# A hybrid pooling / neighbourhood-attention block: the MLP's second-half token operands are written down in three pieces between the early block products instead of in one place

## The chip, the cores and the metric

The kernel runs on one core of one Trainium2 chip. The metric is the device time of one execution in microseconds (us); lower is better. All times inside a run are counted from the start of the span, the stretch from the first to the last instruction that the hardware profiler recorded. The engines are called PE (TensorE matrix products; PEld is its weight load), DVE (VectorE), ACT (ScalarE), POOL (GpSimd) and SP (SyncE, which here only issues transfers).

## The reference

One layer of a diffusion trunk, all in float32, on 1024 tokens of width 1024 with 256 context tokens:

```
h = modulate(rmsnorm(x)); u, q, k, v = h @ w_in
mix = concat(pool_mixer(u), neighbourhood_attention(q, k, v, context)) @ w_out
x = x + gt1 * rmsnorm(mix)
h = modulate(rmsnorm(x), shift2, scale2)             # 1024 x 1024
y = square(relu(h @ w_mlp_in)) @ w_mlp_out           # 1024 x 4096 x 1024
x = x + gt2 * rmsnorm(y)
```

The part around the change is the first MLP product, `h @ w_mlp_in`, and what is just ahead of it.

## The kernel before, in words

Every float32 product is made of three products of rounded operands: an operand is split into a high part (an ACT copy to fp32r, line 143) and a low part (a DVE subtraction, line 144), and `three` (lines 168 to 170) adds high*high, high*low and low*high into one PSUM bank. A split of a 128x1024 page is one ACT cast and one DVE subtraction of that size; a split of a weight tile is one of each, of 128x512.

The first MLP product is done with Strassen's scheme in Winograd's form. The token matrix is cut into four blocks (two token halves, two feature halves) and the weights into four, and seven block products take the place of eight. The token operands have names. `B11` and `B21` come from the first token half (`first_half`). The other five, `T2`, `T1`, `T3`, `B22`, `T4`, need the second token half and are written by `second_half(names)`: two pages each, with subtractions by lines 770 to 775, then a split of each page into `th` (high) and `tl` (low) by `token_part`. In the profile the five carry the names `thT`/`tlT` (for T2, T1, T3, T4) and `thB`/`tlB` (for B22; also for B11 and B21).

The 32 columns of 128 hidden features are worked in 16 pairs p. For p below EARLY = 6 the two products that need only `B11` and `B21` come early: for each group of two pairs, `first_sum` makes x = A11 * B11 in a PSUM bank `phx` (12 matmuls) and copies it to `s1` (line 898, ACT), and `second_sum` adds A12 * B21 into the same bank (12 matmuls more) and squares its positive part (lines 840 and 841, ACT). So the order on PE is x0, x1 with B11, x0, x1 with B21, then the 32 transposes of the second token half (line 737), then x2, x3 and x4, x5 in the same manner. A second sum can't start before its own first sum's copy to `s1` is done, since it changes the bank. After these, `block_pair(p)` does the other five products of a pair, of 12 matmuls each: y with T2 (bank `phy`), z with T1 (`phz`), v with T3 (`phv`), then z with B22 and v with T4 added into their banks. Between z's two products ACT copies the bank out (line 934), and between v's two DVE reads it (line 937). The five weight operands S2, S1, S3, S4, A22 of a pair are made just ahead by `weight_parts`: four DVE combinations (line 813) and five splits.

The order of PE's instructions is fixed by `in_order`. The other engines' queues are ordered when the program is built, by a scheduler that goes by the order in which the code names the instructions and by when it thinks that each can start; the hardware then runs each engine's queue strictly in that order. The instructions of `T2` are held in the written order on ACT and DVE by another `in_order`, and those of block pair 0 may not come before them (`issue_after`). Weight tiles rotate through 8 buffers (`whl`), raw weights through 4 (`wraw`), pages through 33 (`act`), and the small tiles `s1`, `r11`, `u2`, `c22` through 7.

The place of the change:

```
for p in range(0, EARLY, 2):
    ... xs[q], early[q] = first_sum(q) for both q; then second_sum(q, xs[q]) for both
    if p == 0:
        with in_order(ET.Activation, ET.DVE) as made_first:
            second_half(("T2",))
        second_half(("T1", "T3", "B22", "T4"))
```

Of the kernel before, what the change touches and what calls it, by code (L numbers as in the profile page):

```python
# [79 lines left out]
def hybrid_block(ctx, tc, x, ctx_in, w_mod, b_mod, gp1, gp2, w_in, pool_w, rpb, w_out, w1, w2, vectors,  # L80
# [17 lines left out]
    def page(name, dt=F32):  # L98
        return act.tile([P, 1024], dt, tag="pg", name=name)


    @contextmanager
    def in_order(*engines):
        block = nc.cur_bb
        n = len(block.bb.instructions)
        last = {}
        yield last
        assert nc.cur_bb is block
        for i in block.bb.instructions[n:]:
            if i.engine in engines:  # L110
                if i.engine in last:
                    tc.add_manual_dep(i, last[i.engine].name,
                                      mybir.DependencyInfo(mybir.DependencyClass.NoSync, mybir.DependencyReason.DATA),
                                      reason="order")
                last[i.engine] = i
# [564 lines left out]
    with tc.tile_pool(name="ps2", bufs=8, space=PSUM) as ps2:  # L680
# [4 lines left out]
      with ExitStack() as tmp2:  # L685
# [45 lines left out]
        def normal_pair(b, kp, both=True):  # L731
            f = page(f"nf{b}_{kp}")
            for o in range(2):
                k = 2 * kp + o
                pt = bank(f"px{b}_{k}")
                for i in range(4):
                    nc.tensor.transpose(pt[:, i * P : (i + 1) * P], mp1[4 * b + i][:, k * P : (k + 1) * P], ident)
                fo = f[:, o * 512 : (o + 1) * 512]
                if b and o and both:
                    nc.vector.tensor_scalar(fo, pt, a2[:, k : k + 1], s2[:, k : k + 1], mul, add)  # L740
                else:
                    nc.scalar.activation(fo, pt, AF.Identity, bias=s2[:, k : k + 1], scale=a2[:, k : k + 1])
            return f

        def token_part(name, kp, f):
            hi, lo = page(f"th{name}_{kp}", F32R), page(f"tl{name}_{kp}", F32R)
            split(f, hi, lo)
            tok[name, kp] = hi, lo
# [9 lines left out]
        def second_half(names):  # L758
            if not held:
                nf = dict((kp, normal_pair(1, kp, kp % 2 == 0)) for kp in (0, 2, 1, 3))  # L760
                nf = [nf[kp] for kp in range(4)]
                held["b12"], held["B22"] = nf[:2], nf[2:]
                held["T1"], held["T2"] = [[page(f"t{i}_{kp}") for kp in range(2)] for i in (1, 2)]
            b12, b22, b21 = held["b12"], held["B22"], [plain[0, 2 + kp] for kp in range(2)]
            for name in names:
                for kp in range(2):
                    t1, t2 = held["T1"][kp], held["T2"][kp]
                    src = {"T1": t1, "T2": t2, "T3": b12[kp], "B22": b22[kp], "T4": b21[kp]}[name]
                    if name == "T2":
                        nc.vector.tensor_tensor(t1, b12[kp], plain[0, kp], sub)  # L770
                        nc.vector.tensor_tensor(t2, b22[kp], t1, sub)
                    elif name == "T3":
                        nc.vector.tensor_tensor(src, b22[kp], src, sub)
                    elif name == "T4":
                        nc.vector.tensor_tensor(src, src, t2, sub)
                    token_part(name, kp, src)
# [86 lines left out]
        def lookahead(gens, n):  # L863
            ahead = []
            for g in gens:
                for w in g:
                    ahead.append(w)
                    if len(ahead) > n:
                        yield ahead.pop(0)
            yield from ahead  # L870
# [8 lines left out]
        def sequence():  # L879
            for p in range(NPAIR):  # L880
                yield from weight_parts(p, ("S2", "S1", "S3", "S4", "A22") if p < EARLY else
                                        ("A11", "S2", "S1", "S3", "A12", "S4", "A22"))
# [7 lines left out]
        def first_sum(p):  # L890
            x = bank(f"phx{p}")
            step(x, "B11", True)
            if p in (EARLY - 2, EARLY - 1):
                o = (p - EARLY + 2) * 512
                s1 = two_sums[:, o : o + 512]
            else:
                s1 = part(f"s1_{p}")
            nc.scalar.copy(s1, x)  # L898
            return x, s1

        def second_sum(p, x):
            step(x, "B21", False)
            r11 = part(f"r11_{p}")
            squared(x, r11)
            defer(keep, "A11", p, r11)
            return r11
# [13 lines left out]
        def block_pair(p, ahead):  # L920
            sa, sb = page(f"sa{p}"), page(f"sb{p}")
            if p < EARLY:
                s1, r11 = early[p], sb[:, 512:]
                nc.sync.dma_start(r11, kept("A11", p))
            else:
                x, s1 = first_sum(p)
            y = bank(f"phy{p}")
            step(y, "T2", True)
            u2 = part(f"u2_{p}")
            nc.vector.tensor_tensor(u2, y, s1, add)  # L930
            z = bank(f"phz{p}")
            step(z, "T1", True)
            c22 = part(f"c22_{p}")
            nc.scalar.copy(c22, z)
            v = bank(f"phv{p}")
            step(v, "T3", True)
            nc.vector.tensor_tensor(c22, v, c22, add)
            nc.vector.tensor_tensor(c22, c22, u2, add)  # L938
            squared(c22, c22)
            defer(keep, "A22", p, c22)  # L940
            if p >= EARLY:
                r11 = second_sum(p, x)
            ahead()
            step(z, "B22", False)
            c12 = part(f"c12_{p}")
            nc.vector.tensor_tensor(c12, z, u2, add)  # L946
            squared(c12, c12)
            defer(combine_hidden, p, r11, c12, c22, sa, sb)
            ahead()
            step(v, "T4", False)  # L950
            c21 = part(f"c21_{p}")
            nc.vector.tensor_tensor(c21, v, u2, add)
            squared(c21, c21)
            defer(keep, "A12", p, c21)
            defer(combine_last, p, c21, sa, sb)
# [69 lines left out]
        with in_order(ET.PE) as first:  # L1025
            for p in range(0, EARLY, 2):
                both = [q for q in (p, p + 1) if q < EARLY]
                xs = {}
                for q in both:
                    xs[q], early[q] = first_sum(q)  # L1030
                for q in both:
                    second_sum(q, xs[q])
                if p == 0:
                    with in_order(ET.Activation, ET.DVE) as made_first:
                        second_half(("T2",))
                    second_half(("T1", "T3", "B22", "T4"))
            parts = lookahead([sequence()], 4)
            with tc.issue_after(made_first[ET.Activation]), tc.issue_after(made_first[ET.DVE]):
                block_pair(0, lambda: None)
            for p in range(1, NPAIR - 1):  # L1040
                block_pair(p, lambda: None)
# [145 lines left out]
```

## Time and profile before

| | |
|---|---|
| time, median of 3 runs (lowest to highest) | 1126.92 us (1125.63 to 1127.53) |
| profiled execution: its time | 1126.66 us |
| profiled execution: its span | 1124.9 us, 14398 instructions |
| mean granted TensorE clock | 0.985 |
| PE busy | 1075.7 us, 96% |
| DVE busy | 696.4 us, 62% |
| ACT busy | 511.1 us, 45% |
| share of PE in the chain that ended last | 83% |

The busy shares are means over the whole span. The work around the change lies from about 493 us (first early product) to 552 us (end of block pair 0). A timeline row gives the start, the duration, the engine, the line, the operation and its operands and, in brackets, how long the engine had stood idle before and what released it. PE's matmuls are pipelined: one lasts 0.39 us, while a new one starts every 0.227 us. Operations on ACT and DVE overlap in the same way: a 128x512 cast of 0.62 us holds ACT for 0.52 us until the next one starts, a 128x1024 cast of 1.04 us for 0.95 us; a 128x512 subtraction of 0.69 us holds DVE for 0.60 us, one of 128x1024 (1.22 us) for 1.14 us.

### The profile page before, as it was taken

What the parts mean: (1) busy time and instruction counts of PE and PEld (TensorE: products, weight loads), DVE (VectorE), ACT (ScalarE), POOL (GpSimd) and SP (SyncE); (2) the same over time, 40 slices, a digit from 0 to 9 for tenths busy, and PEclk for the clock granted to TensorE, in tenths of its full rate; (3) what the DMA queues carried; (4) which work ended last, traced back from release to release, by engine and by line L of the source; (5) the groups of instructions that cost most, each with busy time, mean ns of one, the idle gap of its engine ahead of it and who ended that gap; (6) DMA issues with size and microseconds to landing.
All of it is one profiled execution on the core that took longest, in us unless ns stands there. A gap on an engine that the chain in (4) does not pass through costs nothing.

```text
span 1124.9 us, 14398 instructions
## 1 busy us (share of the span) xinstructions
PE 1075.7 (96%) x5456; PEld 865.8 (77%) x5456; DVE 696.4 (62%) x1089; ACT 511.1 (45%) x848; POOL 61.6 (5%) x109
## 2 busy tenths in 40 slices
PE   5979999998999999998999999999999999999996
PEld 3667887785677778886888888888878888888885
DVE  4432654624788832579888767675477667556575
ACT  4373112313777732477555455554454334334441
POOL 1020000004220000220000000000000000000001
PEclk9989999998999999998999999999999999999998
DMA  9911863224000001852664535353587666555546
GB/s 285 312 50 37 276 231 113 92 95 143 20 20 2 5 16 48 240 172 75 217 212 165 186 127 173 130 173 112 208 322 277 252 244 223 180 194 187 188 172 202
DMA packets 94265, 179.32 MB, mean 159 GB/s; under 512 B 6898, under 2 KB 39154, under 8 KB 94196
## 3 DMA queue, kind: packets, MB, share of 16 engines
q1 hardware_dynamic: 76644, 144.80, 39.2%
q10 hardware_dynamic: 16272, 29.40, 7.0%
q0 software_dynamic: 1280, 4.21, 1.1%
q8 instruction: 43, 0.70, 0.3%
q14 instruction: 26, 0.21, 0.1%
HBM read 140.62 MB, written 37.76 MB: 159 GB/s over the span
## 4 chain that ended last, share of the span: by engine, by line
PE 83%; DVE 5%; ACT 4%; DMA 4%; issue 2%; POOL 2%; SPq 0%; ACTq 0%; DVEq 0%; POOLq 0%
PE S L586 3%; PE po L650 3%; PE pyv L170 3%; PE pyz L170 3%; PE pyz L169 3%; PE pyv L169 3%; PE pyv L168 3%; PE pyz L168 3%; PE T L624 3%; PE phz L170 3%; PE phz L168 2%; PE phz L169 2%; PE phv L170 2%; PE phv L168 2%; PE phv L169 2%; PE pyx L169 2%
## 5 line engine op out<-in xcount | busy, mean ns | idle before, releaser
L840 ACT ACTIVATE c<-c 128x512 f32<-128x512 f32 x48 | 30.4, 632 | 58.5 <-DVE c L938 24.0
L608 ACT ACTIVATE sp<-sp,nm 128x640 f32<-128x640 f32 (+1 forms) x64 | 51.5, 805 | 11.3 <-DVE nm L600 11.3
L168 PE MATMUL phx<-thB,wpA 128*128 128x512 f32 x128 | 51.1, 400 | 5.6 <-ACT s L898 5.6
L144 DVE TENSOR_TENSOR wpS<-S,wpS 128x512 fp32r<-128x512 f32 x64 | 43.7, 686 | 13.8 <-ACT wpS L143 13.8
L600 DVE CUSTOM_DVE_ANT_0 sp<-S,tab 128x640 f32<-128x640 f32 (+1 forms) x56 | 42.9, 802 | 14.3 <-PE S L586 14.3
L625 ACT COPY pt<-T 128x512 f32<-128x512 f32 x64 | 37.1, 579 | 31.1 <-PE T L624 27.9
L169 PE MATMUL phx<-tlB,wpA 128*128 128x512 f32 x128 | 50.7, 396 | 0.0
L170 PE MATMUL phx<-thB,wpA 128*128 128x512 f32 x128 | 50.5, 395 | 0.0
L143 ACT CAST wpS<-S 128x512 fp32r<-128x512 f32 x64 | 39.3, 615 | 23.3 <-PE phv L170 10.3
L624 PE MATMUL T<-ident,sp 128*128 128x128 f32 x256 | 37.1, 285 | 2.8 <-DVE px L631 2.7
L624 PEld LDWEIGHTS T<-ident,sp 128*128 128x128 f32 x256 | 28.1, 143 | 14.7 <-issue 7.3
L139 POOL TENSOR_TENSOR ry<-vy,nhalf 128x1 f32<-128x1 f32 x8 | 4.4, 550 | 612.1 <-DVE vy L137 612.1
L615 DVE TENSOR_SCALAR sp<-sp,ri 128x640 f32<-128x640 f32 (+1 forms) x64 | 35.4, 553 | 2.3
L586 PE MATMUL S<-kT,q 64*128 64x384 f32 (+1 forms) x128 | 31.9, 525 | 3.2 <-DVE nm L600 3.1
L841 ACT ACTIVATE c<-c 128x512 f32<-128x512 f32 x48 | 30.3, 632 | 10.0 <-DVE sa L911 9.2
L168 PEld LDWEIGHTS phx<-thB,wpA 128*128 128x128 f32 x128 | 24.6, 192 | 11.5 <-ACT s L898 6.4
L713 DVE TENSOR_TENSOR mp<-pw,Ga 128x512 f32<-128x512 f32 x16 | 11.0, 689 | 35.0 <-ACT jo L130 35.0
L946 DVE TENSOR_TENSOR c<-phz,u 128x512 f32<-128x512 f32 x16 | 11.1, 691 | 32.4 <-PE phz L170 32.4
L563 POOL TENSOR_TENSOR tab<-msk,U 128x128 f32<-128x128 f32 x48 | 24.8, 554 | 71.1 <-DMA U<-in_rpb 71.1
L170 PEld LDWEIGHTS phx<-thB,wpA 128*128 128x128 f32 x128 | 24.6, 192 | 5.3
L169 PEld LDWEIGHTS phx<-tlB,wpA 128*128 128x128 f32 x128 | 24.6, 192 | 5.1
L130 ACT ACTIVATE jo<-pw 128x512 f32<-128x512 f32 x16 | 9.6, 598 | 40.4 <-PE pw L170 40.4
(893 smaller groups left out, 3281.3 us busy)
## 6 DMA issues: line engine op xcount, KB each, us to landing
b<-in_w SPq DMA_DIRECT2D x64, 512.0 KB, 4.1
hrS<-hdS SPq DMA_DIRECT2D x32, 512.0 KB, 4.8
hrA<-hdA SPq DMA_DIRECT2D x24, 512.0 KB, 4.7
wm<-in_w_mod SPq DMA_DIRECT2D x16, 512.0 KB, 9.7
wa_0w<-in_w SPq DMA_DIRECT2D x16, 512.0 KB, 4.8
wa_1w<-in_w SPq DMA_DIRECT2D x16, 512.0 KB, 4.2
hdA<-c ACTq DMA_DIRECT2D x32, 256.0 KB, 2.1
hdS<-sa ACTq DMA_DIRECT2D x32, 256.0 KB, 2.9
```

The costliest lines, as they stand in the source:

```text
L143: nc.scalar.copy(hi, src)
L144: nc.vector.tensor_tensor(lo, src, hi.bitcast(F32), sub)
L168: nc.tensor.matmul(ps, ahi, bhi, start=first, stop=False, skip_group_check=more)
L169: nc.tensor.matmul(ps, ahi, blo, start=False, stop=False, skip_group_check=more)
L170: nc.tensor.matmul(ps, alo, bhi, start=False, stop=last, skip_group_check=more)
L586: nc.tensor.matmul(S[e][:, c0 : c0 + keys.shape[1]], q[hs, cols], keys[hs], start=True, stop=True)
L600: nc.vector.tensor_tensor_reduce(out=to, in0=s, in1=bt, scale=1.0, scalar=BIG, op0=add, op1=ALU.min, accum_out=nm)
L608: nc.scalar.activation(sp, sp, AF.Exp, bias=least[i, e], scale=-1.0, accum_out=su)
L615: nc.vector.tensor_scalar_mul(probs[i, e], probs[i, e], ri)
L624: nc.tensor.transpose(t[:, c * P : (c + 1) * P], probs[i, e][:, c * P : (c + 1) * P], ident)
L625: nc.scalar.copy(turns[i][0][:, e], t.rearrange("p (i t) -> p i t", i=4))
L650: nc.tensor.matmul(po[e * HD : (e + 1) * HD, (m % 4) * P : (m % 4 + 1) * P], v[:, f : f + HD], pt[:, e, c] if c < 4 else px[:, e], start=( ...
```

## The change

`second_half` is called three times. After x0 and x1 it writes `T2` only, as before; after x2 and x3 it writes `T1` and `T3`; after x4 and x5 it writes `B22` and `T4`. No instruction is added or taken away, and the pages are handed out in the same order.

```
                 if p == 0:
                     with in_order(ET.Activation, ET.DVE) as made_first:
                         second_half(("T2",))
-                    second_half(("T1", "T3", "B22", "T4"))
+                else:
+                    second_half(("T1", "T3") if p == 2 else ("B22", "T4"))
```

In the built program PE's queue is the same. ACT's queue before, from the cast of T3's second page on (thB22 and thT4 stand for one page each, s4 and s5 for the copies of line 898 of x4 and x5, r4 and r5 for lines 840 and 841 of x4 and x5, "cast S2(0)" for the weight cast of operand S2 of pair 0):

```
before: thT3, cast S2(0), thB22, cast S1(0), thB22, thT4, thT4, s4, s5, cast S3(0), cast S4(0), cast A22(0), r4 840,
        cast S2(1), r4 841, cast S1(1), r5 840, cast S3(1), r5 841, cast S4(1), c0 copy (934), cast A22(1), ...
after:  thT3, cast S2(0), s4, s5, thB22, cast S1(0), cast S3(0), thB22, r4 840, thT4, r4 841, thT4, r5 840,
        cast S4(0), r5 841, cast A22(0), cast S2(1), c0 copy (934), cast S1(1), cast S3(1), cast S4(1), cast A22(1), ...
```

And DVE's ("low X" is the subtraction of line 144 for X, "S2(0)" the combination of line 813 for that weight operand):

```
before: S1(0), low T1, S2(0), low T3, low T3, low S2(0), low B22, low S1(0), low B22, low T4, low T4, S3(0), S4(0),
        S1(1), low S3(0), low S4(0), low A22(0), S2(1), S3(1), S4(1), low S2(1), ..., u0 (930), ...
after:  S1(0), low T1, S2(0), low T3, low T3, low S2(0), S3(0), S4(0), low B22, low S1(0), low B22, low T4, low S3(0),
        low T4, S1(1), low S4(0), u0 (930), low A22(0), S2(1), S3(1), S4(1), low S2(1), low S1(1), low S3(1), c0 (937), ...
```

Further ahead on DVE, the low part of x5's second weight tile (`wpA`) stands four places earlier and the first of T4's two subtractions (line 775) three places later. On SP one load of pair 2's raw weights (`wa_0w`) stands ahead of the load of pair 0's kept result (line 924, `sb`) and not behind it. From block pair 2 on the queues are the same.

## The prediction

> **What bounds the kernel now.** I read the page first: PE is busy for 96% of the span and carries 83% of the chain that ended last, so time can only come from PE's idle stretches, or from stretches in which its clock is down. Then the list of waits, for PE alone, from 500 to 540 us, where the change lies (us in total, times, longest):
>
> ```profile
> PE phx L168 <- ACT s L898: 5.6, 2, 5.2
> ```
>
> One stretch of 5.2 us: a matmul into `phx` waited for a copy of line 898. PE's timeline shows it. Each early product is 12 matmuls; those from 493.18 and from 508.15 us count up to x5's first sum ending at 524.58, so the matmul at 529.97 is the first of x4's second sum:
>
> ```profile
> 524.35 0.39 PE L170 MATMUL phx<-thB,wpA 128*128 128x512 f32 x1
> 529.97 0.80 PE L168 MATMUL phx<-thB,wpA 128*128 128x512 f32 x1 [5.22 <-ACT s L898]
> 530.56 0.63 PE L169 MATMUL phx<-tlB,wpA 128*128 128x512 f32 x1
> ...
> 535.03 0.39 PE L168 MATMUL phx<-thB,wpA 128*128 128x512 f32 x1
> ...
> 537.77 0.39 PE L168 MATMUL phy<-thT,wpS 128*128 128x512 f32 x1
> ```
>
> The idle time is not all of it: x4's second sum takes from 529.97 to 535.03, 5.06 us, x5's after it 2.74. The windows of one us each tell why (last three columns: granted clock, DMA share, GB/s):
>
> ```profile
> 526.00:527.00 1.00, 0.00 (x0) 0.00 (x0) 1.00 (x2) 1.00 (x3) 0.00 (x0) 1.00 0.00 0
> 528.00:529.00 1.00, 0.00 (x0) 0.00 (x0) 1.00 (x2) 1.00 (x2) 0.00 (x0) 0.50 0.00 0
> 534.00:535.00 1.00, 1.00 (x4) 0.82 (x3) 1.00 (x3) 0.86 (x2) 0.00 (x0) 0.62 0.63 157
> 535.00:536.00 1.00, 1.00 (x6) 0.79 (x5) 1.00 (x2) 0.60 (x1) 0.00 (x0) 1.00 0.99 350
> ```
>
> The clock fell to half at about 528 and came back at 534.7. Why was the copy late? x4's first sum had ended by 522. ACT's timeline shows its copy and x5's (the last row) queued behind casts for `second_half`:
>
> ```profile
> 522.24 2.01 ACT L143 CAST thT<-nf 128x1024 fp32r<-128x1024 f32 x2
> 524.51 0.62 ACT L143 CAST wpS<-S 128x512 fp32r<-128x512 f32 x1 [0.26 <-DVE S L813]
> 525.03 1.04 ACT L143 CAST thB<-nf 128x1024 fp32r<-128x1024 f32 x1
> 525.98 0.61 ACT L143 CAST wpS<-S 128x512 fp32r<-128x512 f32 x1
> 526.50 1.04 ACT L143 CAST thB<-nf 128x1024 fp32r<-128x1024 f32 x1
> 527.45 1.99 ACT L143 CAST thT<-nf 128x1024 fp32r<-128x1024 f32 x2
> 529.34 1.06 ACT L898 COPY s<-phx 128x512 f32<-128x512 f32 x2
> ```
>
> So the limit here is the order of ACT's queue, not its speed. From 530 to 800 us PE is busy throughout in every window (of 5 us up to 565, of 20 us from 560).
>
> **What the change does to ACT's queue.** No instruction is added or removed; the built queues (shown with the change) tell what moves. s4 and s5 now stand right behind the cast of S2(0). What is ahead of that cast is the same, so it starts at 524.51, if DVE gives it S2(0) as before. DVE's queue ahead of S2(0) differs by the earlier low part of x5's weight tile. It needs ACT's cast at 509.93 to 510.59, so DVE goes on at 510.63 and not at 509.87, and reaches the low part of T2's second page at 519.59 rather than 519.37. But the next one, the low part of T1's first page, waits in both kernels for its cast, which ends at 520.87. From there DVE is on its old times: S1(0) at 522.05, S2(0) at 523.79.
>
> Then s4 at 524.51 + 0.52 = 525.03. Before, PE started 0.63 us behind the start of this copy (529.34 to 529.97), so now x4's second sum starts at **525.66 instead of 529.97: 4.31 us gained**. PE's gap is 525.66 - 524.58 = 1.08 us.
>
> **The clock.** In the trace one gap of such a size, far from others, left the clock at 1.00: 1.41 us at 401.54, after which the first matmul took 0.34 us to the next, the rest 0.23:
>
> ```profile
> 401.54 0.50 PE L168 MATMUL pw<-wo_2h,mix 128*128 128x512 f32 x1 [1.41 <-DVE mix L657]
> 401.88 0.40 PE L169 MATMUL pw<-wo_2l,mix 128*128 128x512 f32 x1
> 402.12 0.39 PE L170 MATMUL pw<-wo_2h,mix 128*128 128x512 f32 x1
> ```
>
> So I count x4's second sum at 0.34 + 11 x 0.227 = 2.83 us in place of 5.06, 2.23 us gained, and x5's at 2.72 in place of 2.74, 0.02 gained. It ends at 531.21, and y0 starts there instead of at 537.77. Sum: 4.31 + 2.23 + 0.02 = **6.56 us**.
>
> [...]
>
> **Is what was moved back in time for its users?** What stood ahead of s4 (B22's and T4's casts, S1(0)) is now behind it, and y0 comes 6.56 us earlier, so the cover of DVE's and ACT's work shrinks. I lay it out by spacings of the trace (0.52 and 0.95 us for a cast of 512 and 1024 on ACT, 0.60 and 1.14 for DVE), in the built order.
> - ACT: s5 525.55, thB22 526.07, S1(0) 527.02, S3(0) 528.00 (waits for DVE's S3(0), 527.27 + 0.68), thB22 528.52, r4 529.47, thT4 529.97, r4's square 530.92, thT4 531.44, r5 532.39, S4(0) 532.89, r5's square 533.41, A22(0) 533.93. The two issues of kept results stand behind casts and wait for nothing there.
> - DVE, without a gap: low S2(0) 526.67, S3(0), S4(0), low B22 528.47, low S1(0) 529.61, low B22 530.21, low T4 531.35, low S3(0) 532.49, low T4 533.09, S1(1) 534.23, low S4(0) 534.83, u0 535.43 (y0 is done at 534.1), low A22(0) 536.03, S2(1) 536.63 to 537.31. Each finds its cast done.
> - PE wants S1(0) at 533.93 (there at 530.3), S3(0) at 536.65 (533.2), S4(0) and B22 at 539.37 (535.5), A22(0) and T4 at 542.09 (536.7), S2(1) for y1 at 544.81 (539.1).
>
> The new wait with the least room: c0's copy (line 934), which must be out of bank z before z's second product at 539.37, is queued on ACT behind the cast of S2(1), which waits for DVE's S2(1), which stands behind u0. It starts at 537.35 + 0.52 = 537.87 and ends at 538.46: 0.87 us to spare. The read of line 937 ends at 540.93, for v's second product at 542.09: 1.1 us to spare. So these cost nothing. If that cover were gone: some DVE rows at 541 to 544 us lie 0.72 apart, not 0.60. With all 11 small instructions from 522.05 to S2(1) at that, 1.3 us more, PE would lose 1.3 - 0.87 = 0.4 us. The other bound is a gain: nothing, for PE can't start a product before the one ahead of it.
>
> SP's swap is free: `wa_0w` of pair 2 waits for S3(0) (527.95) and was issued at 533.12 before; the `sb` load behind it went out at 528.62 once low B22 had ended (now 529.7) and is wanted by line 910 only after c12 is squared, past 543. Pair 2's `wa_1w` goes out when low A22(0) is done (536.12 before, 536.8 now) and took 3.7 us; DVE asks for it behind line 937, past 541.
>
> **Where the gain could go.** Behind y0, PE has no wait over 0.9 us up to the end (at 821 us, for a DVE row on `b_2l`), and what feeds it is released by PE's own progress. So y0's shift should reach the end whole: 1126.66 - 6.56 = 1120.1 for the profiled execution. That stood 0.26 us under the median, so **1126.92 - 6.56 = 1120.4 us**. A measurement of this kernel can tell 0.2%, 2.25 us, from no change.
>
> **Rivals.**
> 1. *The clock falls all the same.* Against: the gap at 401.54. For: from 266 to 272 us three gaps of 1.4 to 1.6 us stood close together and the windows show 0.50 from 272 to 282. Here the gap ahead is of 0.36 us at 501.5, 23 us earlier. The price is the 2.23 us: 1122.6. [...]
> 2. *Slower: c0's copy becomes the wait.* The chain z's second product <- c0's copy <- S2(1)'s cast <- S2(1) <- u0 on DVE costs PE one for one from the moment when S2(1) ends later than 537.31 + 0.87 = 538.2. [...] For: DVE is busy without a gap from 520.9 on. [...]
> 3. *The gain is given back.* The second MLP product's first loads run with a DMA share near 1.0 from 820 to 850 us, and PE waits 0.9 us there. If that stretch were tied to a fixed time, the wait would grow by up to 6.56 us and leave 1126.9. Against: its loads go out as buffers come free.
> 4. *The change doesn't do what it says*: the scheduler could have left the casts ahead of s4. The built queue excludes that.
>
> **How the numbers follow.** The forecast 0.78, rival 1 0.12, rival 2 0.05, rival 3 0.05. The forecast and rival 1 are faster by over 0.2%, 0.90; rival 3 is within it, 0.05; rival 2 slower, 0.05. The range: at the low end the whole gap goes as well, 1.08 + 0.11 us more, 1119.2, less 0.4 for the scatter of runs (1125.63 to 1127.53); at the high end rival 1's 1122.6 with DVE's 0.4 and some scatter: 1118.8 to 1123.3.
>
> **What would show it.** In the profile after: s4 at about 525.0 right behind a `wpS` cast, PE's gap 1.1 us instead of 5.2, clock 1.00 from 524 to 536, y0 at 531.2, no PE wait from there to 560, and y1 at 544.8. A gap ahead of z's second product (539.4) would be rival 2; a clock of 0.50 with a short gap rival 1; the same shift at 800 us and none at the end rival 3. I am wrong if y0 is early and the total is not.

## The result, and the profile after

The changed kernel takes 1120.39 us (median of 6 runs, 1120.0 to 1121.47) against 1126.44 us for the kernel before (6 runs): a ratio of 0.9942, 95% interval 0.9932 to 0.9952. That is faster by 6.05 us or 0.58%, where 1120.4 was forecast.

PE's waits from 500 to 540 us, in the profile after (total, times, longest):

```profile
PE phx L168 <- ACT s L898: 1.2, 2, 0.9
```

The same two waits are there; the longer one is 0.9 us instead of 5.2. PE's timeline after, from the end of x5's first sum to the start of y0:

```profile
525.61 0.39 PE L170 MATMUL phx<-thB,wpA 128*128 128x512 f32 x1
526.92 0.50 PE L168 MATMUL phx<-thB,wpA 128*128 128x512 f32 x1 [0.92 <-ACT s L898]
527.25 0.40 PE L169 MATMUL phx<-tlB,wpA 128*128 128x512 f32 x1
...
532.49 0.39 PE L168 MATMUL phy<-thT,wpS 128*128 128x512 f32 x1
```

A next matmul could have started at 525.61 + 0.23 = 525.84, so PE lost 1.08 us, and x4's and x5's second sums take 5.57 us together where they took 7.80. A one-us window inside the gap and one behind it (last three columns: granted clock, DMA share, GB/s), in the profile after:

```profile
526.00:527.00 1.00, 0.08 (x1) 0.09 (x1) 1.00 (x2) 1.00 (x3) 0.00 (x0) 1.00 0.00 0
528.00:529.00 1.00, 1.00 (x6) 0.84 (x5) 1.00 (x2) 0.82 (x2) 0.00 (x0) 1.00 0.00 0
```

The clock stays at 1.00. ACT's timeline after shows s4 and s5 (one row) right behind the cast of S2(0), and B22's first page behind them:

```profile
525.76 0.62 ACT L143 CAST wpS<-S 128x512 fp32r<-128x512 f32 x1 [0.26 <-DVE S L813]
526.28 1.06 ACT L898 COPY s<-phx 128x512 f32<-128x512 f32 x2
527.24 1.06 ACT L143 CAST thB<-nf 128x1024 fp32r<-128x1024 f32 x1
```

All times here lie about 1.3 us later than I had worked out. That shift was there before anything that the change touches: x0 starts at 494.57 us after, at 493.18 before, and 1.2 us of it arose already by 28 us, where PE's second group of modulation matmuls (`pm`) started at 28.21 instead of 27.04. In that execution the one-us windows from 24 to 27 us show a granted clock of 0.50, and the matmuls ahead of the group started 0.43 us apart; in the kernel before they show 1.00 and 0.23 us. So two profiled spans, 1124.9 and 1119.6, are 5.3 us apart, and the stretches between fixed matmuls compare the kernels better. For each of the profiled executions of this study, from PE's timeline and the span, in us, each stretch from the first matmul of one product to the first of the other:

| kernel | x0 at | x2 to y0 | y0 to y1 | y1 to y2 | y2 to the end |
|---|---|---|---|---|---|
| before | 493.18 | 29.62 | 13.60 | 13.60 | 559.93 |
| changed | 494.57 | 23.09 | 13.60 | 13.60 | 559.91 |
| changed, again | 493.11 | 23.10 | 13.60 | 13.60 | 559.81 |
| e1: T1, T3 back | 494.57 | 23.08 | 13.60 | 13.60 | 559.90 |
| e2: one place, later | 493.84 | 29.37 | 13.60 | 13.60 | 559.94 |
| e3: T3 too | 496.44 | 21.87 | 13.60 | 13.60 | 559.89 |
| e3's kernel, again | 494.56 | 21.87 | 13.61 | 13.60 | 559.93 |
| e4: all four late | 492.59 | 21.88 | 13.60 | 13.78 | 559.86 |
| e4's kernel, again | 494.52 | 21.85 | 13.60 | 13.75 | 559.85 |
| e5: warm | 492.51 | 27.40 | 13.60 | 13.60 | 559.93 |
| e6: control | 494.20 | 23.07 | 13.60 | 15.14 | 559.94 |
| e7: low T4 twice more | 494.02 | 23.09 | 15.23 | 15.27 | 559.89 |
| e8: five times more | 493.91 | 23.09 | 20.58 | 13.60 | 559.87 |

The last column is the same in all of them within 0.13 us: what is won by y2 reaches the end whole. The x0 column spreads over 4 us with no order in it that fits an edit, and whole times scatter with it.

### The profile page after: what moved, and what is told of

Its sections match the earlier page's. It is cut to its first block, busy times and chain, and to the rows that moved or that the text cites. A ratio compares the mean times of both kernels' runs of the same rounds, so it can differ in the third digit from the quotient of the medians.

```text
span 1119.6 us, 14393 instructions
## 1 busy us (share of the span) xinstructions
PE 1073.9 (96%) x5456; PEld 863.4 (77%) x5456; DVE 695.1 (62%) x1089; ACT 510.5 (46%) x848; POOL 61.8 (6%) x109
## 4 chain that ended last, share of the span: by engine, by line
PE 84%; ACT 4%; DVE 4%; DMA 3%; issue 2%; POOL 2%; SPq 1%; DVEq 0%; POOLq 0%; ACTq 0%
PE S L586 3%; PE po L650 3%; PE pyz L168 3%; PE pyv L168 3%; PE pyv L169 3%; PE pyz L169 3%; PE pyv L170 3%; PE pyz L170 3%; PE T L624 3%; PE phv L168 2%; PE phz L168 2%; PE phv L170 2%; PE phz L170 2%; PE phz L169 2%; PE phv L169 2%; PE pyx L169 2%
```

## The experiments

**Which of the moved operands counts (e1, e2).** Theory A: s4 no longer waits behind B22's and T4's casts. Theory B: the writing is spread over three places. The first edit puts T1 and T3 back beside T2:

```
                     with in_order(ET.Activation, ET.DVE) as made_first:
                         second_half(("T2",))
-                else:
-                    second_half(("T1", "T3") if p == 2 else ("B22", "T4"))
+                second_half({0: ("T1", "T3"), 2: (), 4: ("B22", "T4")}[p])
```

> T1 and T3 are put back behind x0 and x1, beside T2; only B22 and T4 stay behind x4 and x5. Theory A (the time comes from B22's and T4's four casts no longer standing ahead of s4 on ACT): ACT's built queue is that of the changed kernel, so the time is too: about 6.1 us under the kernel before, PE's gap ahead of x4's second sum 1.1 us. Theory B (the gain comes from spreading the writing of operands over three places): T1 and T3 are half of what was moved, so about half of the gain goes, 3 us under the kernel before.

Measured: 1120.32 us (1118.87 to 1121.56), ratio to before 0.9941 (0.9928 to 0.9955); x2 to y0 in 23.08 us, as in the changed kernel. Nothing of the gain went. In ACT's timeline of this kernel s4 and s5 (one row) stand right behind the cast of S2(0) again:

```profile
525.67 0.62 ACT L143 CAST wpS<-S 128x512 fp32r<-128x512 f32 x1 [0.26 <-DVE S L813]
526.19 1.07 ACT L898 COPY s<-phx 128x512 f32<-128x512 f32 x2
```

The second writes all four in one place, one step later than the kernel before: `{0: (), 2: ("T1", "T3", "B22", "T4"), 4: ()}`.

> All four operands are written in one place, behind x2 and x3. Theory A: ACT's built queue is that of the kernel before, B22's and T4's casts ahead of s4: the time of the kernel before within 0.1%, gap 5.4 us, clock down to 0.50 at 528 us. Theory B: the operands are written in two places rather than one: some 2 to 3 us faster than before.

Measured: 1126.56 us, ratio 1.0002 (0.9993 to 1.0011). ACT's timeline of this kernel shows the two copies behind T4's two casts, and PE's what that costs:

```profile
527.97 1.99 ACT L143 CAST thT<-nf 128x1024 fp32r<-128x1024 f32 x2
529.86 1.06 ACT L898 COPY s<-phx 128x512 f32<-128x512 f32 x2
```

```profile
530.49 0.80 PE L168 MATMUL phx<-thB,wpA 128*128 128x512 f32 x1 [5.22 <-ACT s L898]
```

The wait is back at 5.22 us. So of the three places only the last one acts: T1 and T3 may stand behind x1 or behind x3, and B22 and T4 have to be named behind x4 and x5, so that the scheduler puts s4 and s5 ahead of their casts. Theory B falls.

**The rest of the gap (e3, e4).** Two casts of T3 still stand ahead of S2(0)'s cast and s4. In e3 they are named behind x4 and x5 too (`{0: (), 2: ("T1",), 4: ("T3", "B22", "T4")}`), in e4 T1 as well (`{0: (), 2: (), 4: ("T1", "T3", "B22", "T4")}`).

> T1 behind x2 and x3; T3, B22 and T4 behind x4 and x5. In the built queue s4 stands right behind T1's second cast, and s5 behind S2(0)'s. Theory A: s4 starts at 522.2 us on the times of the kernel before, x4's second sum follows x5's first without a gap, y0 starts at 524.58 + 5.44 = 530.0, 1.19 us ahead of the changed kernel: 7.2 us under the kernel before. Rival: T3's pages come too late for v's product at 535.5 us; by my layout their low parts are done at 527.9, so a wait would have to come from elsewhere: then the changed kernel's time or above.

> T1, T3, B22 and T4 all behind x4 and x5. Theory A: s4 stands ahead of T1's casts, no gap, y0 at 530.0 us as with T3 alone: 7.2 us under the kernel before. The casts and low parts come later than there: my layout has the low part of S4(0) done at 537.8 for z's second product at 538.2, 0.4 us to spare, so up to 1 us may be lost again. Theory B: one place again, so the gain is that of one place, none.

ACT's timeline of e3 shows s4 behind T1's second cast (a DMA issue of ACTq falls beside that):

```profile
524.50 1.03 ACT L143 CAST thT<-t 128x1024 fp32r<-128x1024 f32 x1
524.62 0.33 ACTq L861 DMA_DIRECT2D hdA<-r  x1
525.43 0.58 ACT L898 COPY s<-phx 128x512 f32<-128x512 f32 x1
```

From 510 to 560 us PE waits for nothing, and x2 to y0 takes 21.87 us, 1.22 less than in the changed kernel (1.19 expected). In e4 it is 21.88, and 0.18 us come back between y1 and y2. The whole times, 1120.54 and 1119.54 us (ratios 0.9940, 0.9927 to 0.9953, and 0.9937, 0.9924 to 0.9949), don't part them from the changed kernel: e3's profiled execution started x0 at 496.44. So both were run once more on one chip beside the changed kernel.

> The changed kernel once more, as the neighbour of the next two on the same chip: about 1120.4 us, 23.1 us from x2's first matmul to y0.

> T1 behind x2 and x3, the rest behind x4 and x5, once more. The profiled stretch from x2 to y0 should be 21.9 us again, 1.2 less than in the changed kernel. If that reaches the end, the mean of all its runs lies 1.2 us below the changed kernel's; if something behind y0 takes it back, they are equal and the stretch from y2 to the end is longer by as much.

> T1, T3, B22 and T4 all behind x4 and x5, once more: 21.9 us from x2 to y0, up to 0.2 us more between y1 and y2; the mean of all its runs about 1.0 us below the changed kernel's if the gain reaches the end, none if it is taken back behind y2.

Measured: 1120.40, 1119.62 and 1118.73 us. The mean of all runs is 1120.58 (12 of the changed kernel), 1119.96 (11 of e3's) and 1119.08 (11 of e4's). The stretches repeat to 0.03 us, and nothing comes back behind y2. So PE's 1.2 us are shown. In whole times e4's kernel is ahead of the changed one (by 1.5 us, of which the stretches account for 1.0 to 1.1; runs scatter by 1 to 2), e3's is not told apart (0.6 us, where 1.2 was expected).

**The clock's share (e5).** The kernel before, with PE kept busy in the gap; the rest is as it was:

```
+                if p == 4:
+                    warm, th = bank("pwarm"), tok["B11", 0][0]
+                    for _ in range(16):
+                        nc.tensor.matmul(warm, th[:, :P], th[:, :512], start=True, stop=True)
                 for q in both:
                     second_sum(q, xs[q])
```

> The kernel before with 16 matmuls more of 128x512 between x5's first sum and x4's second, into a bank that nobody reads, from operands that are there; the other engines' queues are those of the kernel before. They take 16 x 0.227 = 3.6 us of PE's idle 5.4 and leave a gap of some 1.8 us, so x4's second sum starts where it did. Theory A: the clock stays at 1.00 and the sum takes 2.8 us in place of 5.06: 2.2 us under the kernel before, which is the clock's share of the gain. Rival: the sum is slow for another reason (its operands, a restart of PE): the time of the kernel before.

PE's timeline of this kernel:

```profile
523.70 3.79 PE L1034 MATMUL pwarm<-thB 128*128 128x512 f32 x16
529.10 0.50 PE L168 MATMUL phx<-thB,wpA 128*128 128x512 f32 x1 [1.61 <-ACT s L898]
529.43 0.40 PE L169 MATMUL phx<-tlB,wpA 128*128 128x512 f32 x1
```

PE still waits for s4, x4's second sum still starts 5.4 us behind x5's first, but its matmuls follow one another at 0.23 us. The windows from 527 to 531 us show 1.00, and x2 to y0 takes 27.40 us, 2.22 less than before (2.23 forecast). The whole time is 1123.80 us, ratio 0.9972 (0.9961 to 0.9983). So work of no use in a gap is worth 2.2 us here, and of the 6.5 us that the change wins the clock is a third.

**The room of c0's copy (e6 to e8).** The prediction's slower rival needs c0's copy (line 934) behind the cast of S2(1), and DVE late. When I add DVE work the scheduler moves the copy ahead of that cast in the built queue, so a control holds ACT's order in block pair 0:

```
-                block_pair(0, lambda: None)
+                with in_order(ET.Activation):
+                    block_pair(0, lambda: None)
```

> The changed kernel with ACT's instructions of block pair 0 held in the order in which the code names them, so that c0's copy stays behind the cast of S2(1) as it does in the changed kernel. The control for the next two: the changed kernel's time, 6.1 us under the kernel before, no wait of PE at z's second product.

Then, on top of the control, the low part of T4's first page is computed n times more (n = 2 in e7, 5 in e8), with the same result:

```
             split(f, hi, lo)
+            for _ in range(n if (name, kp) == ("T4", 0) else 0):
+                nc.vector.tensor_tensor(lo, f, hi.bitcast(F32), sub)
```

> As the control, with the low part of T4's first page computed twice more on DVE (2 x 1.14 = 2.28 us) ahead of u0 and S2(1). Theory A (c0's copy has 0.87 us to spare and then costs PE one for one): PE waits 1.4 us ahead of z's second product: 1.4 us above the control. Rival 1 (there is no room): 2.3 us above it. Rival 2 (DVE's work there is covered anyway): the control's time.

> As the control, with the same low part computed five times more (5.7 us). [...] If the clock holds: 4.8 us above the control.

The control missed its expectation: 1123.06 us, 2.7 above the changed kernel. In its block pair 0 nothing is lost (13.60 us), but held in the written order ACT is late for pair 1, as its list of waits from 540 to 565 us shows:

```profile
PE phz L168 <- ACT c L934: 1.2, 1, 1.2
```

That is c1's copy, and 15.14 us from y1 to y2 tell its price, 1.54 us; the rest of the 2.7 is not in these stretches. So e7 and e8 are read by y0 to y1, which the control leaves alone. PE's timelines of e7 and e8, at z's second product of pair 0:

```profile
541.66 0.50 PE L168 MATMUL phz<-thB,wpS 128*128 128x512 f32 x1 [1.33 <-ACT c L936]
```

```profile
544.40 0.79 PE L168 MATMUL phz<-thB,wpS 128*128 128x512 f32 x1 [4.73 <-ACT c L936]
```

(Line 936 is line 934 in these kernels.) Idle times in brackets count from a matmul's end, 0.16 us behind the point at which the next could have started. So PE lost 1.33 + 0.16 = 1.5 us for 2.28 us of DVE work, 0.8 of room, where 0.87 was worked out; and 4.9 for 5.70. From y0 to y1 e7 takes 1.63 us more than the control: nearest to theory A's 1.4, between it and the 2.3 of rival 1, and far from rival 2's nothing. In e8 the clock fell as well:

```profile
541.00:542.00 1.00, 0.00 (x0) 0.00 (x0) 1.00 (x2) 0.00 (x0) 0.00 (x0) 0.87 0.97 343
542.00:543.00 1.00, 0.00 (x0) 0.00 (x0) 0.97 (x2) 0.00 (x0) 0.00 (x0) 0.50 0.03 9
547.00:548.00 1.00, 1.00 (x4) 0.71 (x4) 1.00 (x2) 0.54 (x1) 0.00 (x0) 0.50 0.45 172
549.00:550.00 1.00, 1.00 (x6) 0.82 (x5) 0.62 (x2) 0.62 (x1) 0.00 (x0) 1.00 0.36 143
```

Its y0 to y1 is 20.58 us, 6.98 more than the control's: the gap's 4.9, where 4.8 (5.7 less the room of 0.87) were expected with the clock held, and 2.1 for the slower matmuls behind it. Its time is 1127.58 us, ratio to before 1.0006 (0.9997 to 1.0015): the whole gain is gone. Whole times tell e7 (1123.34 us) not from the control; there only the stretch speaks.

## Why the prediction was right

- **The gap, 4.31 us.** The place of s4 in ACT's queue was read from the built order, its start from rows: 525.03 worked out, 526.28 in the profile after, which is 525.03 moved by the 1.3 us of that execution's start. PE's gap was to be 1.08 us and is 1.08. That this order is the cause, and not the spreading of the work, is shown by e1 and e2.
- **The clock, 2.23 us.** The sums took 5.57 us (5.55 forecast), and e5 gives 2.22 us for the clock alone. That a gap of 1.08 us leaves the clock at 1.00 was judged from one gap of like size in the trace before; the windows from 524 to 536 us in the profile after bear it out. From what idle time on the clock falls, no run shows; what they do show is below.
- **The stretch.** 6.56 us forecast from 508 us to y0, 6.53 measured. That the median came within 0.1 us of the forecast is partly luck, since runs of one kernel differ by 1 to 2 us: the medians are 6.05 us apart, not 6.56, and that of the kernel before came out 0.48 us below the 1126.92 us from which I had subtracted.
- **The cover.** c0's copy was to end 0.87 us ahead of its use and the cast of S2(1) to start at 537.35. After, in ACT's timeline:

```profile
538.59 0.62 ACT L143 CAST wpS<-S 128x512 fp32r<-128x512 f32 x1 [2.84 <-DVE S L813]
539.11 0.58 ACT L934 COPY c<-phz 128x512 f32<-128x512 f32 x1
```

  That is 537.35 moved by 1.2 us, and the copy ends at 539.69, 0.96 ahead of z's second product at 540.65. The brackets show the chain as described: the cast waits for DVE's S2(1). e7 and e8 show that this room is real and what lies behind it.
- **Nothing late to the end.** PE's only wait behind y0 is again the one at `b_2l`, 0.9 us, and y2 to the end takes 559.91 us (559.93 before). Rival 3, the gain given back, falls by that.
- **The rivals.** The clock did not fall; c0's copy did not become the wait, but does with 2.3 us more of DVE work (e7), and 5.7 us take the whole gain (e8); the built order was what the chip ran.

## What to carry to other kernels

When an engine with a strict queue both feeds the next stage and holds a short copy that PE waits for now, look at which of the two stands first in the built queue: here four casts stood ahead of a copy that PE waited for, though PE first read what they wrote at 545.93 us, 16 us after the last of them, and naming them later in the code moved them behind it. Price the idle time of PE together with the clock that it costs (here 4.31 and 2.23 us), and lay out the moved work against the new due times in the built order; the tightest row of that layout (0.87 us here) is what a further edit must not eat. Where the part ahead of the change scatters by more than the effect, compare stretches between fixed instructions rather than whole times.

## What the runs showed of the hardware

Windows of 0.2 us place the changes of the granted clock. In the kernel before it fell to 0.50 at 67.14, 271.94 and 527.94 us and was back at 1.00 at 77.38, 282.18 and 534.76: at 0.50 for 10.24, 10.24 and 6.82 us. In e2 it fell at 528.00 and rose at 534.82, in e8 at 541.73 and 548.56, in the changed kernel at 23.91 and 27.32: at 0.50 for 6.82, 6.83 and 3.41 us. The falls of the kernel before lie 204.80 and 256.00 us apart. All these lengths are whole multiples of 3.41 us within 0.2%: 1, 2, 3, 60 and 75 times.

PE's gaps, by the idle times in brackets: the clock stayed at 1.00 through 0.92 us (changed), 1.33 (e7), 1.41 (before, up to 401.54), 1.61 (e5) and 1.62 (before, up to 106.78). It fell inside gaps of 5.22 us (before and e2), 4.73 (e8) and 3.05 (before, up to 67.77), at 3.20, 2.73, 2.06 and 2.42 us from the end of the last matmul. For a gap between 1.62 and 3.05 us these rows show no clock.

The length of one gap alone doesn't tell them apart. At 271.94 the clock of the kernel before fell in a gap of 1.51 us, behind two of 1.41 and 1.58 us that end at 267.08 and 269.79; PE was busy for 0.91 us between the last two. In the changed kernel it fell at 23.91 us in a gap of 0.23 us, 0.70 us behind the end of one of 1.42, and in the kernel before the same two gaps, the second up to 24.32 us, left it at 1.00. What decides there is not shown.
